# Second feed-forward product by seven block products, with left sums that pass through DRAM

## The chip, the cores and the metric

The kernel runs on one core of a Trainium2 chip. The time is device microseconds for one execution of the whole program. The core's engines are TensorE (PE, with its weight loads PEld), VectorE (DVE), ScalarE (ACT), GpSimd (POOL) and SyncE (SP), whose queue issues nearly all transfers between DRAM and the on-chip memory (SBUF). Matmuls write to eight banks of PSUM.

## What is computed

One encoder block: a mixer (windowed attention and a gated delta rule, side by side), then a feed-forward part with a squared ReLU, then a last RMSNorm. All in float32.

```python
h = h + jnp.concatenate([attn, gdn], axis=-1) @ w_out[l]
hn = _rmsnorm(h, norm_ffn_w[l])
h = h + jnp.square(jax.nn.relu(hn @ w_ffn_in[l])) @ w_ffn_out[l]
return _rmsnorm(h, norm_final_w)
```

There are 1024 tokens, a model width of 1024 and a feed-forward width of 4096. The two feed-forward products take about half of the time; the change lies in the second and in what joins it to the first.

## The kernel before

A float32 product is made of three matmuls. `split` (L111) divides an operand into a high part, a cast by ScalarE (L115), and a low part, the operand less its high part, subtracted by GpSimd (L116). `mm3` (L118) issues high x high, high x low and low x high into one PSUM bank (L120, L121, L122).

The first feed-forward product is already made by seven block products of halves. It runs over 16 groups `g` of 256 feed-forward columns. `columns` makes a group's operands one group ahead (sums S1 to S4 on VectorE, L1016 to L1024, then splits into the tags wh, wl and sc); `pair_products` issues the products P1, P2, P6, P5, P7, P3, P4, each of 12 matmuls of 128x512, so 84 per group. A group's banks are all psA or all psB, by turns. Copies and adds out of PSUM are ScalarE's (L1045) and VectorE's (L1040). Of each group four blocks of 128 feed-forward rows by 512 tokens result; `store_act` (L1048) squares the ReLU of each in one VectorE instruction (L1049) and stores it (L1050) to `ad` in DRAM.

The second product (`ffn2`) runs over 16 groups of 256 feed-forward rows. `load_second` loads a group's two rows of `ad` and two of the weight, 512 KB each (L1093), splits them, and keeps them in tag pg (group 0: in wh, wl and sc, so that it is ready while the first product still runs). For each of eight token tiles and each half of the columns six matmuls follow, and VectorE adds the bank into the residual `h[t]` (L1117). That is 16 x 8 x 2 x 2 x 3 = 1536 matmuls. `h` is loaded from DRAM at the seam (L1235). In the last group `finish` (L1134) normalises and stores each token tile; the last tile has a chain of its own.

Tiles come from pools with a tag and a number of buffers: pg has 28 (of 4 KB a partition), pt 12 (2 KB), wr and sc 4, wh and wl 3, psA and psB 4 banks each. The framework sets each engine's order of instructions at build time, by a timeline that it estimates; on the chip each engine runs its list in order. A transfer on SP waits in that list for the data it stores and for the buffer it fills, and holds those behind it.

Of the kernel before, what the change touches and what calls it, by code (L numbers as in the profile page):

```python
# [30 lines left out]
C_GQ, C_GK, C_GV, C_Z, C_AB = 768, 1280, 1792, 2304, 2816  # L31

# [41 lines left out]
class Block:  # L74
# [987 lines left out]
    def pair_products(self, g, ops):  # L1062
        tag = "psB" if "early" in ops else ("psA", "psB")[g % 2]
# [4 lines left out]
        self.store_act(g, 0, 0, self.add_to(b, p1))  # L1068
# [5 lines left out]
        if "early" in ops:  # L1074
            d, c, x7 = ops["early"]
            self.store_act(g, 1, 1, self.add_to(w, x7))
            self.store_act(g, 0, 1, self.add_to(c, w))
        else:
            d = self.ps(tag)
            self.product(d, ops, "P7")  # L1080
            self.store_act(g, 1, 1, self.add_to(d, w))
# [6 lines left out]
    def load_pair(self, src, mks):  # L1088

        out = []  # L1090
        for i in range(2):
            raw = self.wr((P, D))
            self.nc.sync.dma_start(out=raw, in_=src(i))  # L1093
            h, l = mks[2 * i](dt=F32R), mks[2 * i + 1](dt=F32R)
            for half in range(2):
                sl = slice(half * HALF, (half + 1) * HALF)
                self.split(raw[:, sl], h[:, sl], l[:, sl])
            out.append((h, l))
        return out

    def load_second(self, g):
        m1, m2 = ((self.wh, self.wl, self.sc, self.wh), (self.wl, self.sc, self.wh, self.wl)) if g == 0 else ((self.pg,) * 4,) * 2
        a = self.load_pair(lambda i: self.ad[2 * g + i], m1)
        return a, self.load_pair(lambda i: self.io["w_ffn_out"][0, (2 * g + i) * P:(2 * g + i + 1) * P, :], m2)

    def ffn2(self, a, w2, tiles, last):
        nc = self.nc
        for t in tiles:
            tk = slice(t * P, (t + 1) * P)
            end = last and t == tiles[-1]  # L1110
            ss, rs = self.small((P, 2)), self.small((P, 1))
            halves = [slice(0, HALF), slice(HALF, D)]
            for nh, sl in enumerate(halves):
                ps = self.ps(("psA", "psB")[nh])
                for i in range(2):
                    self.mm3(ps, a[i][0][:, tk], a[i][1][:, tk], w2[i][0][:, sl], w2[i][1][:, sl], i == 0, i == 1)
                nc.vector.tensor_tensor(out=self.h[t][:, sl], in0=self.h[t][:, sl], in1=ps, op=ALU.add)  # L1117
                if end:
                    scr = self.pt((P, HALF), BF16)
                    nc.scalar.activation(out=scr, in_=self.h[t][:, sl], func=AF.Square, accum_out=ss[:, nh:nh + 1])  # L1120
            if end:
                nc.vector.tensor_tensor(out=ss[:, 0:1], in0=ss[:, 0:1], in1=ss[:, 1:2], op=ALU.add)
# [141 lines left out]
```

## Time and profile before

| | us |
|---|---|
| median of three timed runs | 1295.6 (1295.33 to 1300.9) |
| the profiled execution | 1294.7 |
| its span, first to last instruction | 1293.0 |
| TensorE busy | 1244.8 |
| VectorE busy | 820.7 |
| GpSimd busy | 559.7 |
| ScalarE busy | 490.2 |

The first feed-forward product lies at about 630 to 939 us of the span, the second from there to 1285. Busy times are averages over stages of different kinds, so a stage is read by its own window, and a series of matmuls by the distance of their starts: the time of one matmul in the trace overlaps with the next.

### The profile page before, as it was taken

What the parts mean: (1) busy time and instruction counts of PE and PEld (TensorE: products, weight loads), DVE (VectorE), ACT (ScalarE), POOL (GpSimd) and SP (SyncE); (2) the same over time, 40 slices, a digit from 0 to 9 for tenths busy, and PEclk for the clock granted to TensorE, in tenths of its full rate; (3) what the DMA queues carried; (4) which work ended last, traced back from release to release, by engine and by line L of the source; (5) the groups of instructions that cost most, each with busy time, mean ns of one, the idle gap of its engine ahead of it and who ended that gap; (6) DMA issues with size and microseconds to landing.
All of it is one profiled execution on the core that took longest, in us unless ns stands there. A gap on an engine that the chain in (4) does not pass through costs nothing.

```text
span 1293.0 us, 18542 instructions
## 1 busy us (share of the span) xinstructions
PE 1244.8 (96%) x6674; PEld 1005.8 (78%) x6674; DVE 820.7 (63%) x1505; ACT 490.2 (38%) x1119; POOL 559.7 (43%) x490
## 2 busy tenths in 40 slices
PE   6999998999899999999799999999999999999997
PEld 5778776877777778787578888888888888888886
DVE  4667676872489886765886566576355555555556
ACT  6455688145556561215532232232321212121203
POOL 5364222333423242224765554565573636353512
PEclk9999999999899999999899999999999999999999
DMA  6134445424856576132143332332852323232303
GB/s 231 50 120 130 115 155 174 133 77 100 209 162 161 161 277 223 42 106 98 49 139 104 117 111 94 122 107 98 285 195 65 114 82 112 84 103 93 98 1 130
DMA packets 102044, 162.44 MB, mean 126 GB/s; under 512 B 8867, under 2 KB 62240, under 8 KB 101953
## 3 DMA queue, kind: packets, MB, share of 16 engines
q1 hardware_dynamic: 93252, 156.77, 37.5%
q0 software_dynamic: 8448, 4.20, 1.8%
q8 instruction: 52, 0.85, 0.3%
q14 instruction: 39, 0.32, 0.1%
q10 hardware_dynamic: 253, 0.30, 0.1%
HBM read 109.81 MB, written 50.91 MB: 124 GB/s over the span
## 4 chain that ended last, share of the span: by engine, by line
PE 67%; DVE 3%; issue 1%; ACT 1%; DMA 0%; POOL 0%; POOLq 0%; DVEq 0%; ACTq 0%; SPq 0%
PE psA L120 10%; PE psA L122 10%; PE psA L121 10%; PE psB L120 8%; PE psB L122 8%; PE psB L121 8%; PE psB L792 4%; PE psA L580 2%; PE psA L569 2%; PE psA L540 1%; PE psA L541 1%; DVE pt L1040 0%; DMA pg<-in_w_out 0%; DVE pg L211 0%; PE psB L756 0%
## 5 line engine op out<-in xcount | busy, mean ns | idle before, releaser
L116 POOL TENSOR_TENSOR pg<-wr,pg 128x512 fp32r<-128x512 f32 x120 | 151.4, 1299 | 164.5 <-issue 160.4
L120 PE MATMUL psA<-pg,wh 128*128 128x512 f32 x416 | 168.0, 405 | 2.7 <-ACT pt L454 2.1
L122 PE MATMUL psA<-pg,wl 128*128 128x512 f32 x416 | 166.9, 401 | 0.0
L121 PE MATMUL psA<-pg,wh 128*128 128x512 f32 x416 | 166.6, 401 | 0.3 <-POOL pg L945 0.3
L115 ACT CAST pg<-wr 128x512 fp32r<-128x512 f32 x120 | 64.8, 618 | 248.9 <-PE psB L121 234.6
L116 POOL TENSOR_TENSOR wl<-wr,wh 128x512 fp32r<-128x512 f32 x48 | 76.6, 1618 | 160.7 <-ACT wh L115 153.2
L1117 DVE TENSOR_TENSOR pg<-pg,psA 128x512 f32<-128x512 f32 x128 | 87.7, 687 | 82.3 <-PE psA L122 82.3
L1117 DVE TENSOR_TENSOR pg<-pg,psB 128x512 f32<-128x512 f32 x128 | 87.7, 687 | 81.2 <-PE psB L122 81.2
L120 PEld LDWEIGHTS psA<-pg,wh 128*128 128x128 f32 x416 | 79.3, 191 | 22.1 <-ACT pt L454 2.4
L121 PEld LDWEIGHTS psA<-pg,wh 128*128 128x128 f32 x416 | 79.3, 191 | 20.4 <-issue 0.9
L122 PEld LDWEIGHTS psA<-pg,wl 128*128 128x128 f32 x416 | 79.2, 190 | 18.5
L120 PE MATMUL psA<-pg,pg 128*128 128x512 f32 x240 | 93.4, 389 | 0.0
L121 PE MATMUL psA<-pg,pg 128*128 128x512 f32 x240 | 93.4, 389 | 0.0
L120 PE MATMUL psB<-pg,pg 128*128 128x512 f32 x240 | 93.4, 389 | 0.0
L121 PE MATMUL psB<-pg,pg 128*128 128x512 f32 x240 | 93.4, 389 | 0.0
L122 PE MATMUL psA<-pg,pg 128*128 128x512 f32 x240 | 93.4, 389 | 0.0
L122 PE MATMUL psB<-pg,pg 128*128 128x512 f32 x240 | 93.4, 389 | 0.0
L1049 DVE SCALAR_TENSOR_TENSOR pt<-pt 128x512 f32<-128x512 f32 x64 | 90.0, 1407 | 1.1
L115 ACT CAST wh<-wr 128x512 fp32r<-128x512 f32 x80 | 47.0, 623 | 111.7 <-DVE wr L1018 42.7
L116 POOL TENSOR_TENSOR wl<-wr,wl 128x512 fp32r<-128x512 f32 x32 | 53.5, 1673 | 66.3 <-ACT wl L115 66.3
L1040 DVE TENSOR_TENSOR pt<-psA,pt 128x512 f32<-128x512 f32 x39 | 26.7, 686 | 56.1 <-PE psA L122 37.2
L116 POOL TENSOR_TENSOR wh<-wr,wh 128x512 fp32r<-128x512 f32 x32 | 43.1, 1351 | 42.7 <-ACT wh L115 42.7
(374 smaller groups left out, 3024.9 us busy)
## 6 DMA issues: line engine op xcount, KB each, us to landing
wr<-in_w_ffn_in SPq DMA_DIRECT2D x32, 512.0 KB, 3.9
ad<-pt SPq DMA_DIRECT2D x64, 256.0 KB, 2.8
wr<-ad SPq DMA_DIRECT2D x32, 512.0 KB, 3.5
wr<-in_w_ffn_out SPq DMA_DIRECT2D x32, 512.0 KB, 3.6
wr<-in_w_in SPq DMA_DIRECT2D x22, 512.0 KB, 4.8
pg<-in_x SPq DMA_DIRECT2D x16, 512.0 KB, 5.0
sc<-kvd SPq DMA_DIRECT2D x14, 512.0 KB, 4.3
kvd<-pt SPq DMA_DIRECT2D x16, 256.0 KB, 2.7
```

Source lines behind the costliest of these rows:

```text
L115: nc.scalar.copy(out=h, in_=raw)
L116: nc.gpsimd.tensor_tensor(out=l, in0=raw, in1=h.bitcast(F32), op=ALU.subtract)
L120: nc.tensor.matmul(ps, wh, xh, start=first, stop=False, skip_group_check=onto)
L121: nc.tensor.matmul(ps, wh, xl, start=False, stop=False, skip_group_check=onto)
L122: nc.tensor.matmul(ps, wl, xh, start=False, stop=last, skip_group_check=onto)
L540: nc.tensor.matmul(ps[:, :width], q[:, g, :], self.kh[kv][:, keys], start=True, stop=False)
L569: nc.tensor.transpose(ps[:, g, :], tiles[g // 2][:, g % 2, j * P:(j + 1) * P], self.ident)
L580: nc.tensor.matmul(ps[64 * kv:64 * kv + 64, :], self.va[:, kb, 64 * kv:64 * kv + 64], pts[kv][j].rearrange("p g q -> p (g q)"), start=j == ...
L792: nc.tensor.matmul(ps[:, h - g.start, :], left(h), right[:, h, :], start=True, stop=True)
L1040: self.nc.vector.tensor_tensor(out=out, in0=in0, in1=in1, op=ALU.add)
L1049: self.nc.vector.scalar_tensor_tensor(out=c, in0=c, scalar=0.0, in1=c, op0=ALU.max, op1=ALU.mult)
L1117: nc.vector.tensor_tensor(out=self.h[t][:, sl], in0=self.h[t][:, sl], in1=ps, op=ALU.add)
```

## The change

The second product is made by seven block products too. The feed-forward rows are taken in four parts `n` of four groups (k = 0 to 3), the tokens and the output columns in halves. One step is one product of one n: four token tiles x four k x three matmuls, 48. There are 4 x 7 steps, so 1344 matmuls.

The left operands of the seven products are three of the activated blocks (a11, a12, a22) and four sums (s1, s2, s4 and a11 - a21): seven per group. They are made in `pair_products`, where the blocks arise. `act` squares the ReLU by two ScalarE passes in place of the one VectorE instruction, VectorE makes the sums, and `keep` stores the seven blocks to `sd` in DRAM, 256 KB each (four before).

In the second product `second_operands` loads, for each step, four raw left blocks from `sd` into pt, splits them with the subtract on VectorE, and splits the four right ones with the subtract on GpSimd; high and low part now share one pg tile. The right sums T1, T2 (at P6), T3 and N4 (at P5) are made by VectorE, in place over the weights or in pt. The weights come in by eight loads of 512 KB per n, to wr, wh, wl and sc (L1120). `second_products` issues a step's matmuls; P6 goes onto P1's bank, P3 onto P5's and P4 onto P7's. The results are added into `h` by VectorE (L1170); P6 is kept apart in `u2` (copied by ScalarE in n = 0), and in the last n GpSimd adds u2 into three quarters of `h`. `prepare(i + 1)` is written ahead of step i; `prepare(0)` stands behind the last group's `pair_products`. The tile that ends last has its chain in `finish_last`.

```diff
...
-    def store_act(self, g, i, half, c):
-        self.nc.vector.scalar_tensor_tensor(out=c, in0=c, scalar=0.0, in1=c, op0=ALU.max, op1=ALU.mult)
-        self.nc.sync.dma_start(out=self.ad[2 * g + i, :, half * HALF:(half + 1) * HALF], in_=c)
+    def act(self, c):
+
+        self.nc.scalar.activation(out=c, in_=c, func=AF.Relu)
+        self.nc.scalar.activation(out=c, in_=c, func=AF.Square)
+        return c
+
+    def keep(self, g, p, t):
+
+        self.nc.sync.dma_start(out=self.sd[g, SECOND.index(p)], in_=t)
...
-            self.store_act(g, 0, 1, self.add_to(c, u2, self.pt()))
+            a21 = self.act(self.add_to(c, u2, self.pt()))
+        self.keep(g, "P4", a22)
+        s1, s2, s4 = self.pt(), self.pt(), self.pt()
+        v.tensor_tensor(out=s1, in0=a21, in1=a22, op=ALU.add)
+        v.tensor_tensor(out=a21, in0=a11, in1=a21, op=ALU.subtract)
+        v.tensor_tensor(out=s2, in0=s1, in1=a11, op=ALU.subtract)
+        self.keep(g, "P5", s1)
+        self.keep(g, "P7", a21)
+        self.keep(g, "P6", s2)
         self.product(d, ops, "P4", False)
-        self.store_act(g, 1, 0, self.add_to(d, u2))
...
+        a12 = self.act(self.add_to(d, u2))
+        v.tensor_tensor(out=s4, in0=a12, in1=s2, op=ALU.subtract)
+        self.keep(g, "P2", a12)
+        self.keep(g, "P3", s4)
...
+    def second_operands(self, n, w2, p):
...
+        for k in range(4):
+            b = w2[k]
+            raw = self.pt()
+            nc.sync.dma_start(out=raw, in_=self.sd[4 * n + k, SECOND.index(p)])
+            s, t = self.pg((P, 2, HALF), F32R), self.pg((P, 2, HALF), F32R)
+            self.split(raw, s[:, 0], s[:, 1], v)
+            if p == "P6":
+                b["T1"] = b["B11"]
+                v.tensor_tensor(out=b["T1"], in0=b["B12"], in1=b["B11"], op=ALU.subtract)
+                b["T2"] = self.pt()
+                v.tensor_tensor(out=b["T2"], in0=b["B22"], in1=b["T1"], op=ALU.subtract)
+            if p == "P5":
+                b["T3"], b["N4"] = b["B12"], b["B21"]
+                v.tensor_tensor(out=b["T3"], in0=b["B22"], in1=b["B12"], op=ALU.subtract)
+                v.tensor_tensor(out=b["N4"], in0=b["B21"], in1=b["T2"], op=ALU.subtract)
+            self.split(b[SECOND_RIGHT[p]], t[:, 0], t[:, 1])
+            left.append(s)
+            right.append(t)
+        return left, right
+
+    def second_products(self, n, p, left, right, banks, last):
...
+        for i in range(4):
+            ps = banks[bank, i] = self.ps(tag) if tag else banks[bank, i]
+            tk = slice(i * P, (i + 1) * P)
+            for k in range(4):
+                self.mm3(ps, left[k][:, 0, tk], left[k][:, 1, tk], right[k][:, 0], right[k][:, 1],
+                         tag is not None and k == 0, k == 3, tag is None)
+            u2 = self.u2[i // 2][:, i % 2]
+            if p == "P6" and n == 0:
+                nc.scalar.copy(out=u2, in_=ps)
+                continue
...
+            nc.vector.tensor_tensor(out=dst, in0=dst, in1=ps, op=ALU.add)
+            if last and p == "P6":
+                for d in (self.h[i][:, hi], self.h[4 + i][:, hi], self.h[4 + i][:, lo]):
+                    nc.gpsimd.tensor_tensor(out=d, in0=d, in1=u2, op=ALU.add)
+            if last and p in ("P3", "P4"):
+                self.finish(i if p == "P3" else 4 + i)
...
             else:
-                nxt = self.load_second(0)
+                w2 = self.load_second(0)
             self.pair_products(g, cols.pop(g))
...
+        prepare(0)
+        for t in range(NT):
             self.h[t] = self.pg((P, D))
             nc.sync.dma_start(out=self.h[t], in_=self.hd[t])
...
+        self.u2 = [self.pg((P, 2, HALF)) for _ in range(2)]
+        for i, (n, p) in enumerate(steps):
+            if i + 1 < len(steps):
+                prepare(i + 1)
...
+            self.second_products(n, p, *ops.pop(i), banks, last)
```

Three places show how the order moves. Line numbers are those of the file that the rows are from: `split` has its cast in L115 and its subtract in L116 before, in L119 and L120 after. The numbers behind a tag tell its buffers apart.

The first is SP's queue at the seam of the two products. Before, the last three stores of group 15 (L1050) stand among the loads of the second product's groups (L1093):

```order
L1050 DMA ad_68<-pt_1482_8501 128x512
L1093 DMA wr_1537_8742<-ad_68 128x1024
L1050 DMA ad_68<-pt_1484_8531 128x512
L1093 DMA wr_1540_8750<-ad_68 128x1024
L1050 DMA ad_68<-pt_1480_8486 128x512
L1093 DMA wr_1543_8758<-in_w_ffn_out 128x1024
L1093 DMA wr_1546_8766<-in_w_ffn_out 128x1024
L1093 DMA wr_1581_8918<-ad_68 128x1024
```

After, the last seven stores of the first product (L1060) come first, pt_1521 being the last activated block (a12) and pt_1528 the sum s4, and behind them the left loads of P1 and P2 (L1132):

```order
L1060 DMA sd_68<-pt_1526_8731 128x512
L1060 DMA sd_68<-pt_1525_8726 128x512
L1060 DMA sd_68<-pt_1527_8732 128x512
L1060 DMA sd_68<-pt_1521_8681 128x512
L1060 DMA sd_68<-pt_1528_8733 128x512
L1132 DMA pt_1529_8758<-sd_68 128x512
L1132 DMA pt_1532_8766<-sd_68 128x512
L1132 DMA pt_1535_8774<-sd_68 128x512
L1132 DMA pt_1538_8782<-sd_68 128x512
L1132 DMA pt_1551_8808<-sd_68 128x512
L1132 DMA pt_1554_8816<-sd_68 128x512
```

All loads of left operands have moved behind the last store of the first product.

The second is ScalarE at the same place. Before, casts for the second product's groups stand around the last copies out of PSUM (L1045):

```order
L1045 COPY pt_1479_8457<-psB_1477_8443 128x512
L115 CAST sc_1469_8421<-wr_1468_8419 128x512 x2
L115 CAST wl_1472_8429<-wr_1471_8427 128x512 x2
L115 CAST pg_1494_8568<-wr_1493_8566 128x512 x2
L1045 COPY pt_1480_8486<-psB_1477_8443 128x512
L115 CAST wh_1475_8437<-wr_1474_8435 128x512 x2
L115 CAST pg_1497_8576<-wr_1496_8574 128x512 x2
L115 CAST pg_1500_8584<-wr_1499_8582 128x512 x2
L115 CAST pg_1503_8592<-wr_1502_8590 128x512 x2
```

After, the ReLU (L1054) and the square (L1055) of the last blocks come, then the casts of P1, a left and a right one by turns:

```order
L1054 ACTIVATE pt_1523_8696<-pt_1523_8696 128x512
L1055 ACTIVATE pt_1523_8696<-pt_1523_8696 128x512
L1054 ACTIVATE pt_1525_8726<-pt_1525_8726 128x512
L1055 ACTIVATE pt_1525_8726<-pt_1525_8726 128x512
L1054 ACTIVATE pt_1521_8681<-pt_1521_8681 128x512
L1055 ACTIVATE pt_1521_8681<-pt_1521_8681 128x512
L119 CAST pg_1530_8760<-pt_1529_8758 128x512
L119 CAST pg_1531_8761<-wr_1510_8621 128x512
L119 CAST pg_1533_8768<-pt_1532_8766 128x512
L119 CAST pg_1534_8769<-wl_1512_8625 128x512
```

The casts of the first operands, right ones (from the weights in wr and wl) among them, now stand behind the square of the last block.

The third is VectorE there. Before, the last add and relu-square of group 15 are followed by the adds of the second product (L1117):

```order
L1040 TENSOR_TENSOR pt_1484_8531<-psB_1481_8488,pt_1480_8486 128x512
L1049 SCALAR_TENSOR_TENSOR pt_1484_8531<-pt_1484_8531 128x512
L1040 TENSOR_TENSOR pt_1480_8486<-psB_1483_8503,pt_1480_8486 128x512
L1049 SCALAR_TENSOR_TENSOR pt_1480_8486<-pt_1480_8486 128x512
L1117 TENSOR_TENSOR pg_1485_8550<-pg_1485_8550,psA_1507_8600 128x512
L1117 TENSOR_TENSOR pg_1486_8552<-pg_1486_8552,psA_1511_8618 128x512
L1117 TENSOR_TENSOR pg_1487_8554<-pg_1487_8554,psA_1515_8636 128x512
```

After, the last sums of the first product (L1099, L1100, L1106) are followed by low parts of left blocks (L120) and right sums (L1137, L1139, L1142):

```order
L1044 TENSOR_TENSOR pt_1521_8681<-psB_1524_8698,pt_1521_8681 128x512
L1099 TENSOR_TENSOR pt_1525_8726<-pt_1520_8651,pt_1525_8726 128x512
L1100 TENSOR_TENSOR pt_1527_8732<-pt_1526_8731,pt_1520_8651 128x512
L1106 TENSOR_TENSOR pt_1528_8733<-pt_1521_8681,pt_1527_8732 128x512
L120 TENSOR_TENSOR pg_1530_8760<-pt_1529_8758,pg_1530_8760 128x512
L120 TENSOR_TENSOR pg_1533_8768<-pt_1532_8766,pg_1533_8768 128x512
L1137 TENSOR_TENSOR wr_1510_8621<-wr_1510_8621 128x512
L120 TENSOR_TENSOR pg_1536_8776<-pt_1535_8774,pg_1536_8776 128x512
L1139 TENSOR_TENSOR pt_1570_8903<-wh_1511_8623,wr_1510_8621 128x512
L1142 TENSOR_TENSOR wr_1510_8621<-wh_1511_8623,wr_1510_8621 128x512
L1137 TENSOR_TENSOR wl_1512_8625<-wl_1512_8625 128x512
L120 TENSOR_TENSOR pg_1539_8784<-pt_1538_8782,pg_1539_8784 128x512
```

and this goes on up to the low part of P2's last left block (pg_1561) and the first adds out of PSUM (L1170):

```order
L1139 TENSOR_TENSOR pt_1582_8936<-sc_1517_8635,wl_1516_8633 128x512
L1142 TENSOR_TENSOR wl_1516_8633<-sc_1517_8635,wl_1516_8633 128x512
L1143 TENSOR_TENSOR sc_1513_8627<-sc_1513_8627,pt_1574_8914 128x512
L120 TENSOR_TENSOR pg_1561_8834<-pt_1560_8832,pg_1561_8834 128x512
L120 TENSOR_TENSOR pg_1568_8898<-pt_1567_8896,pg_1568_8898 128x512
L1143 TENSOR_TENSOR wh_1515_8631<-wh_1515_8631,pt_1578_8925 128x512
L1170 TENSOR_TENSOR pg_1541_8790<-pg_1541_8790,psA_1563_8840 128x512
L1170 TENSOR_TENSOR pg_1542_8792<-pg_1542_8792,psA_1564_8854 128x512
```

Between s4 and the low part of pg_1561, that included, stand 22 instructions with two inputs in SBUF, where before the adds out of PSUM followed at once.

## Rows read from the trace of the kernel before

**Rows 1.** The page: span, busy time by engine, chain that ended last.
```profile
span 1293.0 us, 18542 instructions
PE 1244.8 (96%) x6674; PEld 1005.8 (78%) x6674; DVE 820.7 (63%) x1505; ACT 490.2 (38%) x1119; POOL 559.7 (43%) x490
...
PE 67%; DVE 3%; issue 1%; ACT 1%; DMA 0%; POOL 0%; POOLq 0%; DVEq 0%; ACTq 0%; SPq 0%
```

**Rows 2.** Windows: us; PE, PEld, DVE, ACT, POOL busy; clock; DMA share; GB/s.
```profile
700.00:800.00 100.00, 100.00 (x432) 80.85 (x431) 63.54 (x65) 26.30 (x45) 52.48 (x35) 1.00 0.33 107
1000.00:1100.00 100.00, 100.00 (x443) 82.81 (x442) 50.28 (x74) 21.35 (x40) 50.27 (x40) 1.00 0.32 100
```

**Rows 3.** Timeline of TensorE, first product: start us, us, instruction.
```profile
758.75 0.39 PE L120 MATMUL psA<-pg,wl 128*128 128x512 f32 x1
...
797.81 0.40 PE L120 MATMUL psA<-pg,wl 128*128 128x512 f32 x1
```

**Rows 4.** Timeline of TensorE, end of the second product.
```profile
1269.87 0.39 PE L120 MATMUL psB<-pg,pg 128*128 128x512 f32 x1
...
1283.47 0.39 PE L120 MATMUL psB<-pg,pg 128*128 128x512 f32 x1
...
1284.61 0.39 PE L122 MATMUL psB<-pg,pg 128*128 128x512 f32 x1
```

**Rows 5.** Groups: busy us, mean ns of one, idle before and releaser.
```profile
L116 POOL TENSOR_TENSOR pg<-wr,pg 128x512 fp32r<-128x512 f32 x120 | 151.4, 1299 | 164.5 <-issue 160.4
...
L115 ACT CAST pg<-wr 128x512 fp32r<-128x512 f32 x120 | 64.8, 618 | 248.9 <-PE psB L121 234.6
...
L1117 DVE TENSOR_TENSOR pg<-pg,psA 128x512 f32<-128x512 f32 x128 | 87.7, 687 | 82.3 <-PE psA L122 82.3
```

**Rows 6.** Groups of VectorE in the first product, 700 to 900 us.
```profile
L1049 DVE SCALAR_TENSOR_TENSOR pt<-pt 128x512 f32<-128x512 f32 x41 | 66.3, 1616 | 0.7
```

**Rows 7.** Timeline of VectorE and GpSimd, where two instructions meet.
```profile
741.52 1.74 POOL L116 TENSOR_TENSOR wl<-wr,wl 128x512 fp32r<-128x512 f32 x1 [4.07 <-ACT wl L115]
...
742.02 1.78 DVE L1049 SCALAR_TENSOR_TENSOR pt<-pt 128x512 f32<-128x512 f32 x1
```

**Rows 8.** Timeline at the seam: TensorE, SP's queue, VectorE.
```profile
938.50 0.39 PE L122 MATMUL psB<-pg,sc 128*128 128x512 f32 x1
938.73 0.39 PE L120 MATMUL psB<-wh,sc 128*128 128x512 f32 x1
...
932.23 0.33 SPq L1050 DMA_DIRECT2D ad<-pt  x1
...
938.93 0.69 DVE L1040 TENSOR_TENSOR pt<-psB,pt 128x512 f32<-128x512 f32 x1 [1.57 <-PE psB L122]
939.65 0.69 DVE L1049 SCALAR_TENSOR_TENSOR pt<-pt 128x512 f32<-128x512 f32 x1
```

**Rows 9.** DMA issues: number, KB of each, median us to landing.
```profile
ad<-pt SPq DMA_DIRECT2D x64, 256.0 KB, 2.8
wr<-ad SPq DMA_DIRECT2D x32, 512.0 KB, 3.5
...
pt<-pd SPq DMA_DIRECT2D x16, 256.0 KB, 5.4
```

**Rows 10.** Windows ahead of the first product: TensorE busy, clock, DMA share, GB/s.
```profile
628.00:630.00 2.00, 0.16 (x2) 0.83 0.00 0
630.00:632.00 2.00, 1.39 (x3) 0.50 0.00 0
632.00:634.00 2.00, 2.00 (x6) 0.50 0.57 165
634.00:636.00 2.00, 2.00 (x5) 0.50 0.28 98
636.00:638.00 2.00, 2.00 (x9) 0.96 0.85 263
```

More of the change, by code (lines that the diff above doesn't have):

```diff
@@ L1062, in pair_products @@
     def pair_products(self, g, ops):
+        v = self.nc.vector
         tag = "psB" if "early" in ops else ("psA", "psB")[g % 2]
@@ L1080, in pair_products @@
             self.product(d, ops, "P7")
[L1081 removed]
+            a22 = self.act(self.add_to(d, w))
             self.product(c, ops, "P3", False)
[L1083 to L1099 removed]
@@ L1101, in load_second @@
[L1101 to L1106, printed above, removed]
-        nc = self.nc
[L1108 to L1122, printed above, removed]
-                self.rstd(ss[:, 0:1], rs)
-                hw, o = self.pt(), [self.pt(), self.pt()]
-                nc.gpsimd.tensor_tensor(out=hw, in0=self.h[t][:, halves[0]], in1=self.w_fin[:, halves[0]], op=ALU.mult)
-                nc.scalar.activation(out=o[0], in_=hw, func=AF.Copy, scale=rs)
-                nc.vector.scalar_tensor_tensor(out=o[1], in0=self.h[t][:, halves[1]], scalar=rs,
-                                               in1=self.w_fin[:, halves[1]], op0=ALU.mult, op1=ALU.mult)
-                for nh, sl in enumerate(halves):
-                    (nc.scalar, nc.sync)[nh].dma_start(out=self.io["out"][0, t * P:(t + 1) * P, sl], in_=o[nh])
-            elif last:
-                self.finish(t)
@@ new lines, in second_operands @@
+    def second_operands(self, n, w2, p):
+        nc, v = self.nc, self.nc.vector
+        left, right = [], []
+        for k in range(4):
[17 more added lines that the diff above has]
+        return left, right
@@ new lines, in finish_last @@
+    def finish_last(self, t, ps):
+        nc = self.nc
+        lo, hi = slice(0, HALF), slice(HALF, D)
+        h = self.h[t]
+        ss, rs = self.small((P, 2)), self.small((P, 1))
+        scr, hw, o = self.pt((P, HALF), BF16), [self.pt(), self.pt()], [self.pt(), self.pt()]
+        nc.scalar.activation(out=scr, in_=h[:, hi], func=AF.Square, accum_out=ss[:, 1:2])
+        nc.gpsimd.tensor_tensor(out=hw[1], in0=h[:, hi], in1=self.w_fin[:, hi], op=ALU.mult)
+        nc.vector.tensor_tensor(out=h[:, lo], in0=h[:, lo], in1=ps, op=ALU.add)
+        nc.scalar.activation(out=scr, in_=h[:, lo], func=AF.Square, accum_out=ss[:, 0:1])
+        nc.vector.tensor_tensor(out=hw[0], in0=h[:, lo], in1=self.w_fin[:, lo], op=ALU.mult)
+        nc.vector.tensor_tensor(out=ss[:, 0:1], in0=ss[:, 0:1], in1=ss[:, 1:2], op=ALU.add)
+        self.rstd(ss[:, 0:1], rs)
+        nc.scalar.activation(out=o[0], in_=hw[0], func=AF.Copy, scale=rs)
+        nc.vector.tensor_scalar(out=o[1], in0=hw[1], scalar1=rs, scalar2=None, op0=ALU.mult)
+        for i, sl in enumerate((lo, hi)):
+            (nc.scalar, nc.sync)[i].dma_start(out=self.io["out"][0, t * P:(t + 1) * P, sl], in_=o[i])
```

52 lines of the change are left out of this document (38 added, 14 removed).

## The prediction

> **What bounds the kernel now.** I read the page first: the span is 1293.0 us, TensorE is busy for 96% of it, and the chain that ended last runs for 67% through its matmuls, with no other engine above 3% [rows 1]. Then the windows: in the first feed-forward product as in the second, TensorE is busy for all 100 us at a granted clock of 1.00, while VectorE has 64 and 50 of 100, ScalarE 26 and 21, GpSimd 52 and 50 [rows 2]. So a matmul taken away there is worth its whole pitch, as long as the other engines and the loads keep up. The busy time of one matmul (0.39) isn't its pitch, since matmuls overlap. The pitch is read from two starts: in the first product the first matmul of a psA tile comes again after two groups, 168 matmuls, 39.06 us later, 0.2325 us each [rows 3]. In the second, two matmuls five token tiles (60 matmuls) apart are 13.60 us apart, 0.2267 us each [rows 4]. What sets the two apart that I can see is the tag of the operands: the faster rows have both in pg.
>
> **Removed: matmuls.** The second product has 16 groups x 8 tiles x 2 halves x 2 x 3 = 1536 matmuls now and 4 x 7 x 4 x 4 x 3 = 1344 after. Of the 1536, group 0's 96 lie in other tags: 96 x 0.2325 + 1440 x 0.2267 = 348.7 us. After, all operands are in pg: 1344 x 0.2267 = 304.6 us. That is **-44.1 us**, and -36.2 if they should go at 0.2325.
>
> **Added beside the first product.** Per group of 19.5 us (84 x 0.2325) the change takes four relu-squares off VectorE, 1.62 us each [rows 6], and puts four sums there; ScalarE gets eight passes, at the 0.62 us of a cast of the same size 5.0 us [rows 5]; three more 256 KB stores go out. By the windows VectorE has 12.4 us per group now, so some 12.4 - 6.5 + 4 x 1.62 = 12.4 at the old price and 8.7 at 0.69; ScalarE 5.1 + 5.0 = 10.1. Both lie under 19.5. The load on the DMA queues goes from 107 GB/s [rows 2] to about 107 + 0.79 MB / 19.5 us = 147. None of it is on the path in steady state: a relu-square isn't a reader of PSUM, so the banks come free as before. VectorE's sums wait for ScalarE's squares, though, and the next group's operand sums (S1) stand behind s4 on VectorE. Where a group's operands are made late, as at the start of the stage, that can show: **+2 us** (0 to 5), an allowance, bounded by four dependent waits of 1.24 us.
>
> **The seam between the products.** Now it costs nothing: the last matmul of the first product starts at 938.50, the next TensorE rows follow at the usual pitch, and VectorE's add and relu-square run beside them [rows 8]. After, the order puts the loads of the first left operands on SP behind the last two stores of group 15, and the casts on ScalarE behind that group's last relu and square, though the blocks loaded are those of groups 0 to 3, long written. From the last matmul of group 15: VectorE's add 0.69 [rows 8], relu and square 2 x 0.62 [rows 5], s4 0.69 [rows 8], the store's issue 0.33 [rows 8], a load's landing 3.5 (2.8 to 5.4, [rows 9]; the 3.5 is a load of the same kind of buffer in this stage): 6.5 us idle. Two casts, left then right: 1.24. Then TensorE doesn't run freely, since the operands come one by one from three engines. VectorE has 22 two-input instructions up to the low part of P2's last left block, 22 x 0.69 = 15.2 us alone. Beside them GpSimd makes eight right low parts of 1.30 [rows 5], and a two-input VectorE instruction that meets one of these waits: the relu-square started at 742.02 took 1.78 and not 0.69 because GpSimd's subtract ran until 743.26 [rows 7]. In the mean over 41 of them it was 1.62, that is 0.93 more [rows 6]. With 8 x 0.93 the queue needs 0.62 + 15.2 + 7.4 = 23.2 us from the landing (15.8 with no meeting, 26.2 with 8 x 1.30). TensorE running freely would want that block at its 57th matmul, 1.24 + 57 x 0.2267 = 14.2. So it waits about 9 us in P1 and P2 (1.6 to 12). Last the clock: after TensorE had been nearly idle from 624 to 630 the granted clock was 0.50 for some 5.5 us of work, that is 1.2 instead of 2.4 GHz [rows 10], which would cost 2.75 us; part of it falls into the waits just named, so 2. Sum: 6.5 + 1.24 + 9 + 2 = **+18.7 us** (9 to 25).
>
> **The second product in steady state.** One n is 336 matmuls, 76.2 us. ScalarE: 56 casts x 0.62 = 34.7. GpSimd: 28 x 1.30 = 36.4. VectorE: 28 adds from PSUM x 0.687 = 19.2, which GpSimd doesn't lengthen (the mean over 128 is 687 ns at a GpSimd busy half of the time, [rows 2, 5]), and 44 two-input instructions, 44 x 0.69 = 30.4, plus 28 x 0.93 = 26.0 for the meetings: 75.6 of 76.2. So TensorE covers it, but only just, and unevenly: the 16 right sums of an n stand in the two steps before its P1 and P2. There VectorE has 27 two-input instructions, eight adds and eight meetings, 18.6 + 5.5 + 7.4 = 31.5 us in two steps of 10.9. What helps is that an add of P4 may be some 8 us late before the next P1 wants its bank (the other three tiles of the step come first), and that the operands have 2.25 steps of pg buffers; I allow 1 us for each of three such places, **+3 us** (0 to 8). Loads are 28 x 0.26 MB + 8 x 0.52 MB = 11.5 MB per n, 151 GB/s, against 100 now [rows 2]; up to 263 GB/s were moved in a window [rows 10]. In the last n GpSimd has 12 adds more, 15.6 us, 52 of 76: covered, and no product but the last ones waits for them.
>
> **The tail.** From the last matmul (1284.61, [rows 4]) to the end are 8.4 us now. finish_last has the same chain behind it, add, square, small sum, rstd, scale, store. I take 0 (-0.5 to +0.5).
>
> **The sum.** On the profiled execution: 1294.7 - 44.1 + 2 + 18.7 + 3 = 1274.3 us. That execution is 0.9 under the median of 1295.6, so **1275 us**. About 0.5% can be told from no change, so faster means under 1289.1 and slower over 1302.1.
>
> **Rivals.**
> *The pitch stays at 0.2325.* The high and low parts will share one pg tile, and if the faster pitch comes from something else than the tag, the second product takes 312.5 us: 1275 + 7.9 = 1283. For it: I have only a correlation. Against it: 1440 matmuls hold the faster pitch.
> *VectorE becomes the bound, and the kernel is slower.* If every one of the 28 right low parts of an n blocks VectorE for its full 1.30 us, an n needs 30.4 + 36.4 + 19.2 = 86.0 us against 76.2, 9.8 x 4 = 39 more, 1275 + 39 - 3 = 1311. It passes the time before from 5 us per n on, a meeting price of 1.11 (75.6 is reached at 0.93). For it: the row at 742.02 lost 1.09. Against it: the waits take turns, GpSimd's subtract is held up too (1.74 instead of 1.30, [rows 5, 7]), so fewer meet, and such a VectorE only meets when both have work. The Trainium skill, page "SBUF — State Buffer", section "Who interferes with whom", has a rule for this: a VectorE instruction with two inputs in SBUF and a GpSimd instruction that reads SBUF take a lock, and the later one blocks in full until the other ends. By that rule the full 1.30 is the most that a meeting costs, and this rival its worst case; the row at 742.02 agrees with the rule, its 1.78 being the rest of GpSimd's 1.74 and 0.6 of its own.
> *The first product slows.* If the chain add, relu, square, sums, S1 of the next group ends last in each of 14 groups by 1 us, 1275 - 2 + 14 = 1287. Against it: operands are made a group ahead, and ScalarE and VectorE have a third of each group free.
> *The seam is cheap.* With no meetings there (wait 1.6, the clock's loss inside it): 1275 - 9.4 = 1266; with a landing in 2.8 us and no other allowance 1260.
>
> **How the numbers follow.** The forecast, seam near 19 us and the rest hidden, 0.54; the slow pitch 0.17; VectorE bound 0.09; the first product 0.08; the cheap seam 0.10; 0.02 for what I haven't thought of. The low end of the range is the cheap seam with its bounds, 1260. The high end takes in the pitch rival and the first product's, and the forecast with seam and allowances at their upper bounds (+6 +3 +5 = 1289): 1289. VectorE bound and half of what lies beyond stay out. Faster: 0.54 + 0.17 + 0.10 + half of 0.08 = 0.85; slower 0.08 of VectorE's 0.09; the rest, 0.07, within 0.5%.
>
> **What would show it.** In the profile after: TensorE idle for 6 to 7 us behind group 15 and then with gaps through P1 and P2, ended by VectorE's low parts, at a granted clock that falls to 0.50; 0.2267 us from matmul to matmul in the second product; VectorE's mean for its left low parts between 0.7 and 1.6 us; gaps of TensorE before P1 and P2 of a new n of a microsecond at most; groups of the first product still 19.5 us apart. The prediction is wrong if TensorE waits for VectorE in every n (then the meetings are dearer), if the first product's groups are longer, or if the seam is hidden.

## The result, and the profile after

The changed kernel takes 1278.05 us in the median (1276.52 to 1282.06), against 1295.8 before: ratio 0.986, 95% interval 0.983 to 0.989. The forecast was 1275 in a range of 1260 to 1289. The profiled execution took 1276.97 us, 17.7 less than that of before.

The page of after, the same parts as [rows 1]: span, busy time, the chain that ended last.

```profile
span 1275.3 us, 18723 instructions
PE 1207.9 (95%) x6482; PEld 972.6 (76%) x6482; DVE 860.6 (67%) x1534; ACT 613.6 (48%) x1347; POOL 580.9 (46%) x486
...
PE 22%; DVE 2%; issue 1%; DMA 0%; ACT 0%; SPq 0%; POOLq 0%; DVEq 0%; POOL 0%
```

192 matmul records have gone. TensorE's busy time fell by 36.9 us and the span by 17.7 only, so idle time has come in somewhere. The waits of TensorE from 620 to 960 us and behind that say where (engine, line, who was waited for, us in total, times, longest):

```profile
PE psA L124 <- ACT pg L119: 9.4, 1, 9.4
PE psB L124 <- ACT pt L1049: 2.6, 1, 2.6
...
PE psB L124 <- DVE pt L1044: 1.4, 1, 1.4
...
PE psA L126 <- DVE pg L120: 4.0, 2, 3.2
PE psB L126 <- DVE pg L120: 3.2, 3, 1.3
```

None of these stood in the trace of before. L1049 and L1044 are the copy and the add out of PSUM in group 15; the others lie at the seam and in the three steps behind it. After 986 us TensorE waits for nothing until its last matmul; this window shows most of that stretch (columns as in [rows 2]):

```profile
1030.00:1240.00 210.00, 210.00 (x928) 173.91 (x927) 175.71 (x199) 82.31 (x154) 136.49 (x85) 1.00 0.39 119
```

The pitches are about those of [rows 3, 4]. In the first product a psA tile's first matmul comes again after two groups, 168 matmuls, 39.13 us later (39.06 before); at the end of the second, 39 matmuls take 8.84 us, 0.2267 each:

```profile
758.39 0.39 PE L124 MATMUL psA<-pg,wh 128*128 128x512 f32 x1
...
797.52 0.39 PE L124 MATMUL psA<-pg,wh 128*128 128x512 f32 x1
...
1257.73 0.39 PE L126 MATMUL psA<-pg,pg 128*128 128x512 f32 x1
...
1266.57 0.39 PE L126 MATMUL psA<-pg,pg 128*128 128x512 f32 x1
```

So the gain is where it was expected, and most of the loss is at the seam. Its timeline, SP's queue, ScalarE, TensorE:

```profile
940.92 3.40 SPq L1060 DMA_DIRECT2D sd<-pt  x5
944.41 4.99 SPq L1132 DMA_DIRECT2D pt<-sd  x9
...
948.63 0.62 ACT L119 CAST pg<-pt 128x512 fp32r<-128x512 f32 x1 [6.12 <-DMA pt<-sd]
...
949.83 2.07 PE L124 MATMUL psA<-pg,pg 128*128 128x512 f32 x4 [9.36 <-ACT pg L119]
...
961.89 0.50 PE L126 MATMUL psA<-pg,pg 128*128 128x512 f32 x1 [3.18 <-DVE pg L120]
```

The last matmul of group 15 started at 940.07; five stores fill SP's queue until 944.32, the first load behind them lands after 4.2 us (to the cast that waits for it), and TensorE starts at 949.83, 9.36 us after it fell idle. Then P1 and P2, 96 matmuls, take until 982.50: 32.7 us for 21.8 us of work. VectorE and GpSimd in that stretch:

```profile
949.28 0.69 DVE L120 TENSOR_TENSOR pg<-pt,pg 128x512 fp32r<-128x512 f32 x1 [6.04 <-ACT pg L119]
...
951.61 1.77 DVE L1137 TENSOR_TENSOR wr<-wr 128x512 f32<-128x512 f32 x1
953.30 1.78 DVE L120 TENSOR_TENSOR pg<-pt,pg 128x512 fp32r<-128x512 f32 x1
955.00 1.78 DVE L1139 TENSOR_TENSOR pt<-wh,wr 128x512 f32<-128x512 f32 x1
...
973.95 3.48 DVE L120 TENSOR_TENSOR pg<-pt,pg 128x512 fp32r<-128x512 f32 x2
...
952.79 1.74 POOL L120 TENSOR_TENSOR pg<-wr,pg 128x512 fp32r<-128x512 f32 x1
954.49 1.75 POOL L120 TENSOR_TENSOR pg<-wl,pg 128x512 fp32r<-128x512 f32 x1
```

From 951 to 963 us each engine starts one instruction every 1.70 us, in turn: a two-input VectorE instruction waits for GpSimd's subtract, and the next subtract for it. VectorE's first line here begins its row of 22 up to P2's last low part; the line of 973.95 holds the 22nd, which ended at 975.73, and one more. The granted clock (windows of TensorE: busy, clock, DMA share, GB/s) falls to 0.50 with the idle time and stays there for some matmuls behind it, as in [rows 10]. It does so behind the wait of 2.6 us in group 15 too (first line). At the seam the DMA engines are full:

```profile
930.00:932.00 2.00, 2.00 (x6) 0.50 1.05 407
...
944.00:946.00 2.00, 0.00 (x0) 0.50 1.05 407
...
950.00:952.00 2.00, 2.00 (x5) 0.50 1.05 402
952.00:954.00 2.00, 2.00 (x7) 0.70 1.07 411
...
964.00:966.00 2.00, 2.00 (x6) 0.50 0.97 361
```

For the experiments I use a second measure beside the median. Ahead of the first product all kernels here run the same instructions in the same order, and yet that part ended between 629.8 and 634.5 us in their profiled executions. So the length from the first matmul of the first product to the last matmul of the second, in the profiled execution, compares better where a few us matter.

| kernel | median us | length us | against the changed kernel |
|---|---|---|---|
| before | 1295.8 | 654.0 | +17.5 |
| changed | 1278.05 | 636.5 | |
| sums_only | 1303.8 | 662.6 | (before + 8.6) |
| loads_ahead | 1277.38 | 636.7 | +0.2 |
| right_dve | 1266.94 | 626.2 | -10.3 |
| act_dve | 1275.98 | 633.6 | -2.9 |
| seam_dve | 1273.24 | 629.5 | -7.0 |
| left_pool | 1306.88 | 656.9 | +20.3 |
| hoist | 1272.54 | 630.7 | -5.8 |
| best | 1263.94 | 623.9 | -12.6 |
| dve_act | 1264.08 | | |
| best_queue | 1260.89 | 617.0 | -19.5 |
| own_queue | 1261.69 | 617.0 | -19.5 |

The profiled execution of dve_act ran at a granted clock of 0.56, so it has no length here.

### The profile page after: what moved, and what is told of

It reads as the page before. It is cut to its first block, busy times and chain, and to the rows that moved or that the text cites. A ratio compares the mean times of both kernels' runs of the same rounds, so it can differ in the third digit from the quotient of the medians.

```text
span 1275.3 us, 18723 instructions
## 1 busy us (share of the span) xinstructions
PE 1207.9 (95%) x6482; PEld 972.6 (76%) x6482; DVE 860.6 (67%) x1534; ACT 613.6 (48%) x1347; POOL 580.9 (46%) x486
## 5 line engine op out<-in xcount | busy, mean ns | idle before, releaser
L119 ACT CAST pg<-pt 128x512 fp32r<-128x512 f32 x128 | 76.4, 617 | 165.9 <-PE psA L126 63.5
L120 DVE TENSOR_TENSOR pg<-pt,pg 128x512 fp32r<-128x512 f32 x112 | 133.9, 1217 | 26.3 <-ACT pg L119 25.6
L120 POOL TENSOR_TENSOR wl<-wr,wh 128x512 fp32r<-128x512 f32 x44 | 70.5, 1625 | 153.6 <-ACT wh L119 153.6
L120 POOL TENSOR_TENSOR wh<-wr,wh 128x512 fp32r<-128x512 f32 x32 | 47.1, 1491 | 141.6 <-ACT wh L119 133.9
L1054 ACT ACTIVATE pt<-pt 128x512 f32<-128x512 f32 x64 | 40.4, 632 | 145.4 <-DVE pt L1044 145.4
L124 PE MATMUL psA<-pg,pg 128*128 128x512 f32 x256 | 100.4, 397 | 9.4 <-ACT pg L119 9.4
L126 PE MATMUL psA<-pg,pg 128*128 128x512 f32 x256 | 100.7, 394 | 4.0 <-DVE pg L120 4.0
L125 PE MATMUL psA<-pg,pg 128*128 128x512 f32 x256 | 100.5, 393 | 0.0
L126 PE MATMUL psB<-pg,pg 128*128 128x512 f32 x192 | 74.9, 391 | 3.2 <-DVE pg L120 3.2
L125 PE MATMUL psB<-pg,pg 128*128 128x512 f32 x192 | 74.7, 389 | 0.0
L124 PE MATMUL psB<-pg,pg 128*128 128x512 f32 x192 | 74.7, 389 | 0.0
L1044 DVE TENSOR_TENSOR pt<-psB,pt 128x512 f32<-128x512 f32 x39 | 26.9, 690 | 63.8 <-PE psB L126 38.2
L1044 DVE TENSOR_TENSOR pt<-psA,pt 128x512 f32<-128x512 f32 x39 | 26.7, 689 | 59.2 <-PE psA L126 42.0
L119 ACT CAST wh<-wr 128x512 fp32r<-128x512 f32 x76 | 43.5, 623 | 45.1 <-PE psA L125 24.5
L124 PEld LDWEIGHTS psA<-pg,pg 128*128 128x128 f32 x256 | 49.0, 192 | 19.9 <-ACT pg L119 9.8
L126 PEld LDWEIGHTS psA<-pg,pg 128*128 128x128 f32 x256 | 48.7, 190 | 15.5 <-DVE pg L120 5.3
```

What stands on the lines that cost most here:

```text
L120: (eng or nc.gpsimd).tensor_tensor(out=l, in0=raw, in1=h.bitcast(F32), op=ALU.subtract)
L124: nc.tensor.matmul(ps, wh, xh, start=first, stop=False, skip_group_check=onto)
L125: nc.tensor.matmul(ps, wh, xl, start=False, stop=False, skip_group_check=onto)
L126: nc.tensor.matmul(ps, wl, xh, start=False, stop=last, skip_group_check=onto)
L1044: self.nc.vector.tensor_tensor(out=out, in0=in0, in1=in1, op=ALU.add)
L1054: self.nc.scalar.activation(out=c, in_=c, func=AF.Relu)
```

## The experiments

My theory after the comparison: the seam costs by three things, the queue ahead of the first loads (9.4 us idle), the turns that VectorE and GpSimd take in P1 and P2 (10.9 us), and a last group in which ScalarE's copy stands behind its squares (2.6 us). The rival on the second point: VectorE simply has too many instructions there.

### The first product's part alone: sums_only

To the kernel before, `act`, the four sums and their stores are added; the second product stays.

```diff
-        self.store_act(g, 0, 0, self.add_to(b, p1))
+        a11 = self.act(self.add_to(b, p1))
+        self.half(g, 0, 0, a11)
...
+        v.tensor_tensor(out=s1, in0=a21, in1=a22, op=ALU.add)
+        a31 = self.pt()
+        v.tensor_tensor(out=a31, in0=a11, in1=a21, op=ALU.subtract)
+        v.tensor_tensor(out=s2, in0=s1, in1=a11, op=ALU.subtract)
...
+        v.tensor_tensor(out=s4, in0=a12, in1=s2, op=ALU.subtract)
```

> The kernel before with the changed first product alone: relu and square on ScalarE, four sums a group on VectorE, four more stores a group (eight in all, where the change has seven); the second product as before, from its own buffer, and the sums are read by nobody. My theory: the first product hides this work except at its last group, where in the changed kernel TensorE waited 2.6 us for ScalarE's copy and 1.4 us for an add behind it, so 1297 to 1300 us, 1 to 4 over the kernel before. Rival: the sums and the longer chain cost in every group (1 us each), then 1309 or more.

Measured: 1303.8 us, ratio to before 1.0075 (1.0049 to 1.010), more than expected. TensorE's waits from 900 to 960 us:

```profile
PE psB L120 <- ACT pt L1045: 2.0, 1, 2.0
PE psA L120 <- DVE pg L1143: 1.8, 1, 1.8
PE psA L121 <- POOL wl L116: 1.8, 1, 1.8
PE psB L120 <- ACT sc L115: 0.9, 1, 0.9
```

6.6 of the 8.6 us are waits at the seam, and the groups ahead of it are 0.1 us longer each (19.6 for 19.5). So the rival falls: the sums cost 0.1 us a group and not 1. But the longer chain isn't free at the end of the stage, even where the second product waits for no sum.

### The first loads ahead of the last stores: loads_ahead

```diff
+        if g == DFF // 256 - 1:
+            self.raws = [self.raw_left(0, j, "P1") for j in range(4)]
         self.product(d, ops, "P4", False)
...
-            raw = self.pt()
-            nc.sync.dma_start(out=raw, in_=self.sd[4 * n + k, SECOND.index(p)])
+            raw = self.raws[k] if (n, p) == (0, "P1") else self.raw_left(n, k, p)
```

> The changed kernel, with the four left loads of the first step issued ahead of the last two stores of group 15; nothing else moves. My theory: 6 of the 9.4 us in which TensorE stands idle at the seam are the SP queue (stores waiting for their data, their issues, then the landing); with the blocks there, ScalarE's casts follow its last square at once, so the idle time falls to about 3.5 us and the total to about 1272. Rival: what paces the seam is VectorE's row of instructions behind it, and P1 and P2 end when that ends; it starts earlier too, so this rival only says that part is lost again: 1274 to 1276. Second rival: the loads only find buffers late, and nothing changes, 1278.

Measured: 1277.4 us. SP's queue, ScalarE and TensorE's waits:

```profile
942.80 0.96 SPq L1129 DMA_DIRECT2D pt<-sd  x2
...
947.56 0.62 ACT L119 CAST pg<-pt 128x512 fp32r<-128x512 f32 x1 [3.60 <-DMA pt<-sd]
...
PE psA L124 <- ACT pg L119: 6.8, 1, 6.8
PE psB L126 <- DVE pg L120: 5.2, 3, 1.9
```

The idle time fell by 2.5 us only, not by 6: the loads still stood behind a sum's store, and ScalarE's cast of the first came 4.8 us after its issue, in a stretch in which the DMA engines are full. And what was won was lost: P1 and P2 take 36.7 us and not 32.7. TensorE's waits for VectorE's low parts there are 6.9 us for 6.4, but 34 matmuls for 17 start at the lower clock, 0.43 us apart, and lose 6.6 us for 3.3. The time is the same; length +0.2. That is the first rival's mechanism: VectorE's row sets when P2 ends. Its last low part for P2 ended 35.3 us behind the start of group 15's last matmul here, and 35.7 in the changed kernel.

### No GpSimd in the second product: right_dve, seam_dve

right_dve gives the right low parts to VectorE in all steps; seam_dve in P1 and P2 of the first n alone.

```diff
-            self.split(b[SECOND_RIGHT[p]], t[:, 0], t[:, 1])
+            self.split(b[SECOND_RIGHT[p]], t[:, 0], t[:, 1], v)
```

```diff
-            self.split(b[SECOND_RIGHT[p]], t[:, 0], t[:, 1])
+            self.split(b[SECOND_RIGHT[p]], t[:, 0], t[:, 1], v if n == 0 and p in ("P1", "P2") else None)
```

> The changed kernel with the right low parts too subtracted on VectorE, in all steps, so that GpSimd does none in the second product. My theory: at the seam VectorE and GpSimd hold each other up (1.7 us for an instruction of either by turns), so that without GpSimd VectorE's row, though it has eight instructions more up to P2's last block (30 x 0.6 to 0.69 = 18 to 21 us), ends earlier than now (about 23 us from its start to P2's last low part); P1 and P2 take 26 to 29 us in place of 32.7, total 1271 to 1275. In steady state VectorE has 72 x 0.65 + 19 = 66 of 76 us and TensorE has no gaps. Rival, VectorE's count of instructions decides: eight more make the seam longer by 5 us and each n's VectorE the bound at its first steps: 1283 or more.

Measured: 1266.9 us, ratio to before 0.978 (0.976 to 0.980), better than expected. VectorE's row at the seam of right_dve, and TensorE's waits there:

```profile
951.09 0.68 DVE L120 TENSOR_TENSOR pg<-wr,pg 128x512 fp32r<-128x512 f32 x1
951.69 0.69 DVE L120 TENSOR_TENSOR pg<-pt,pg 128x512 fp32r<-128x512 f32 x1
952.29 0.68 DVE L1137 TENSOR_TENSOR wr<-wr 128x512 f32<-128x512 f32 x1
...
PE psA L124 <- ACT pg L119: 9.8, 1, 9.8
PE psB L124 <- ACT pt L1049: 2.6, 1, 2.6
```

Eight instructions more, one every 0.60 us and not every 1.70, and no wait for a low part is left. From TensorE's start at 951.02 to its last matmul at 1256.96 are 305.9 us; 1344 matmuls at 0.2267 are 304.7. So the theory of the turns holds, and the rival, that the count decides, falls.

> The changed kernel with the right low parts subtracted on VectorE in the first two steps alone (eight instructions); in the 26 later steps GpSimd has them as before. My theory after right_dve: all of its 11 us lie in P1 and P2 of the first n, where VectorE and GpSimd alternate at 1.7 us for each of their instructions, and nothing in the later steps: 1266 to 1269, as right_dve. Rival: meetings cost in every n too, hidden in TensorE's pitch or in short gaps; then this one gives back a part, 1270 to 1275.

Measured: 1273.2 us. It gives back 7.0 us of length and not 10.3: P1 and P2 run without a wait for a low part, and the turns come a step later, in P6, where TensorE waits 3.1 us for low parts (three times). This is the rival's side of the expectation as to the number, though not as to the place: in the later n no wait appears. GpSimd's first subtract in seam_dve shows something else:

```profile
959.30 9.65 POOL L120 TENSOR_TENSOR pg<-pt,pg 128x512 fp32r<-128x512 f32 x1 [40.09 <-ACT pg L119]
...
967.10 0.68 DVE L1143 TENSOR_TENSOR sc<-sc,pt 128x512 f32<-128x512 f32 x1
967.71 0.68 DVE L1170 TENSOR_TENSOR pg<-pg,psA 128x512 f32<-128x512 f32 x1
968.30 1.19 DVE L1139 TENSOR_TENSOR pt<-sc,wl 128x512 f32<-128x512 f32 x1
```

It started into a run of two-input VectorE instructions, each 0.60 us after the last, and took 9.65 us; it ended 1.24 us after VectorE began to read from PSUM (L1170), about its time alone. So engines that meet don't always take turns: here an unbroken run of the one kept the other out. Every trace read here has another such case near 244 us, in the mixer: there a subtract that starts into a run of smaller two-input VectorE instructions takes 6.7 to 7.8 us (6.90 in the changed kernel, in which 17 instructions of VectorE that started later ran ahead of it), and ends 1.2 us behind the run's last.

### All of it on GpSimd: left_pool

```diff
-            self.split(raw, s[:, 0], s[:, 1], v)
+            self.split(raw, s[:, 0], s[:, 1])
```

> The changed kernel with the left low parts subtracted on GpSimd too, 56 an n, so that VectorE has 16 two-input instructions and 28 adds from PSUM. Theory of meetings (a two-input VectorE instruction and a GpSimd subtract don't run at once): an n needs 56 x 1.28 + 16 x 0.6 = 81 us of the two engines by turns against TensorE's 76, 5 x 4 = 20 more, and the seam is longer, 16 low parts of 1.28 ahead of P2's end and not 8: 1295 to 1310. Rival, the engines only share or the counts alone decide: GpSimd needs 71.7 of 76.2 us and VectorE 30: 1275 to 1285.

Measured: 1306.9 us, slower than before, ratio 1.0088 (1.0068 to 1.011).

```profile
PE psA L124 <- DVE pg L1170: 21.1, 4, 10.4
PE psA L124 <- ACT pg L119: 9.5, 1, 9.5
...
DVE wr L1137 <- POOL pg L120: 9.2, 2, 8.8
```

The number is as the theory of meetings gave it, by a somewhat other way. GpSimd is full in the later windows (68.8 of 70 us from 1140 to 1210), its subtract takes 1.39 us and not 1.30, so an n takes 56 x 1.39 = 78 us and not 81; of the 21.1 us, 17 fall in the first two n (6.6 and 10.4), where VectorE's sums wait for GpSimd and the adds out of PSUM stand behind them. That the number came out is partly luck. P1 and P2 take only 2.0 us more than in the changed kernel (34.7 for 32.7), so nearly all of the loss lies behind the seam. Another 7.6 us are lost behind the last matmul (16.3 for 8.7), which the theory didn't have.

### Relu and square back on VectorE: act_dve

```diff
-        self.nc.scalar.activation(out=c, in_=c, func=AF.Relu)
-        self.nc.scalar.activation(out=c, in_=c, func=AF.Square)
+        self.nc.vector.scalar_tensor_tensor(out=c, in0=c, scalar=0.0, in1=c, op0=ALU.max, op1=ALU.mult)
```

> The changed kernel with relu and square again in one VectorE instruction in the place of two ScalarE passes. My theory: the wait of 2.6 us of TensorE in group 15 came from ScalarE's copy standing behind the squares of group 14, and goes, and the seam's chain is shorter by 0.6 us (one instruction of 0.69 for two of 0.63): 1274 to 1276. Rival: VectorE, which meets GpSimd in the first product (1.6 us a relu-square) and has the sums now too, becomes late in every group: 1285 or more.

Measured: 1276.0 us, as expected, though against the changed kernel that is within what runs differ by. In the trace the wait for L1049 is gone and nothing takes its place; the first product is 305.6 us long and not 310.0, so VectorE isn't late there. 2.6 of these 4.4 us are the wait, and 1.6 the matmuls at the lower clock behind it (up to 932.81). At the seam 1.5 of the 4.4 us are lost again.

### The operands of the first step made beside the first product: hoist, best

Group 15 makes P7 and P3 first, so that operand buffers come free, and `prepare(0)` moves ahead of its `pair_products`. best has right_dve and act_dve too.

```diff
                 w2 = self.load_second(0)
+                for _ in self.early(cols[g]):
+                    pass
+                prepare(0)
             self.pair_products(g, cols.pop(g))
...
-        prepare(0)
```

> The changed kernel, but group 15 makes P7 and P3 first, as groups 0 and 1 do, so that eight operand buffers come free early, and the first step's operands are loaded and split while group 15 runs; meetings stay. My theory: the idle time of 9.4 us at the seam goes nearly all, and the low parts of P1 are made beside the first product; P2's row of VectorE and GpSimd is still paced by meetings, so 3 to 6 of the 11 us in P1 and P2 stay: 1263 to 1269. Rival: as with loads_ahead, what is won at the seam is lost in P1 and P2 behind the same row of VectorE: 1274 or more.

> Three edits together: group 15 makes P7 and P3 first and the first step's operands are made beside it (hoist), all low parts of the second product are VectorE's (right_dve), relu and square are one VectorE instruction (act_dve). My theory: the gains add, since they lie in three places, 9 at the seam's idle time, 11 in P1 and P2, 4 in the first product (its length was 310.0 us in the changed kernel and 305.6 in act_dve): 1278 - 24 = 1254, between 1251 and 1259. Rival: VectorE, which then has most of the work beside TensorE, is late in P2 of the first n and takes back a part: 1260 to 1266.

Measured: 1272.5 us in hoist, between its two ranges and nearer the rival's, and 1263.9 in best, in its rival's. The seam itself lost its gap, 2.1 us idle in hoist and none in best, but a wait of 7.5 and 9.6 us stands ahead of P2. In best, SP's queue, ScalarE and TensorE:

```profile
948.46 8.13 SPq L1059 DMA_DIRECT2D sd<-pt  x5
956.64 0.44 SPq L1131 DMA_DIRECT2D pt<-sd  x1
...
960.64 0.62 ACT L119 CAST pg<-pt 128x512 fp32r<-128x512 f32 x1 [17.87 <-DMA pt<-sd]
...
961.83 2.08 PE L124 MATMUL psB<-pg,pg 128*128 128x512 f32 x4 [9.55 <-ACT pg L119]
```

The rival of best named VectorE, and it is SP: P2's left loads stand behind five stores of group 15, and these wait for VectorE's last sums, which the order puts behind adds of P1. The wait had only moved from the first step to the second.

### The loads on a queue of their own: dve_act, best_queue, own_queue

dve_act is right_dve with act_dve. best_queue is best, own_queue is dve_act, and in both the left loads of P1 and P2 of the first n go out on GpSimd's queue, and P2's operands are written ahead of the loads of `h`.

```diff
-            nc.sync.dma_start(out=raw, in_=self.sd[4 * n + k, SECOND.index(p)])
+            (nc.gpsimd if n == 0 and p in ("P1", "P2") else nc.sync).dma_start(out=raw, in_=self.sd[4 * n + k, SECOND.index(p)])
...
+        prepare(1)
         for t in range(NT):
             self.h[t] = self.pg((P, D))
```

> right_dve and act_dve together: in the second product all low parts on VectorE, in the first relu and square in one VectorE instruction; the loads stay where they are. My theory: two places, two gains, 11 from P1 and P2 and 4 from the first product (310.0 to 305.6 us), so 1262 to 1264, and TensorE idle for 9 us at the seam as before. Rival, VectorE is late where it has both: 1267 or more.

> The kernel best, in which TensorE went through the seam without a gap but then stood idle for 9.6 us ahead of P2 of the first n, since P2's left loads stood in SP's queue behind group 15's last stores (948.5 to 956.6) and those behind VectorE; here the eight left loads of P1 and P2 go out on GpSimd's queue, which has nothing else there, and the 4 MB of the residual are issued after them. My theory: the 9.6 us go but for 1 to 3, 1254 to 1258. Rival, the DMA engines are the limit there (share 1.0, 400 GB/s, from 935 to 955 in best) and the loads land as late whatever queue they stand in: 1262 or more.

> dve_act with the eight left loads of P1 and P2 of the first n on GpSimd's queue, and P2's operands written ahead of the loads of the residual; group 15 keeps its order. The loads are free of SP's stores, so the blocks lie there when group 15 ends, and the casts wait only for operand buffers, which P3 of group 15 gives back 2.8 us before its end. My theory: TensorE's idle time falls from 9 to 2 to 4 us and nothing is lost behind it, since VectorE is quick enough there: 1255 to 1259. Rival, DMA engines at the limit: 1261 or more.

Measured: 1264.1, 1260.9 and 1261.7 us. The first is as expected. The other two lie some 3 us above the expected ranges, own_queue in that of its rival, the DMA engines at their limit; part of that is the stretch ahead of the first product, 2.5 and 3.8 us longer in their profiled executions than in that of the changed kernel. Their lengths are both 617.0, 6.9 under best and 9.2 under right_dve. In the medians the queue is worth less, 3.1 us from best and 2.4 from dve_act, and the runs of own_queue and dve_act overlap (1259.9 to 1262.9 and 1260.2 to 1265.1). So its gain rests on the traces. TensorE's waits in own_queue, and the landing of the eight loads on GpSimd's queue (median, us):

```profile
PE psA L125 <- DVE pg L120: 4.6, 2, 2.5
...
PE psB L124 <- DVE pt L1044: 1.4, 1, 1.4
PE psA L124 <- ACT pg L119: 0.4, 1, 0.4
...
pt<-sd POOLq DMA_DIRECT2D x8, 256.0 KB, 6.4
```

The idle time at the seam is 0.4 us. So SP's queue was what held the first loads. Behind that, 4.6 us wait for low parts, which my theory had at nothing, and matmuls at the lower clock lose another 1.2. There the full DMA engines may well have a part: the eight loads took 6.4 us to land, against 3.0 in the median of the changed kernel's 112 left loads, and VectorE stood 3.1 us until a sum's store had landed. What lighter traffic would give isn't shown. In best_queue the edit also moves P2's loads ahead of the residual's, and the two aren't told apart; in the changed kernel they were ahead already. Both are the fastest here by their medians: ratio to before 0.974 (0.972 to 0.976), where dve_act has 0.975 (0.973 to 0.977).

## Why the prediction was right

**The matmuls, -44.1: right.** 1344 at 0.2267; the rival of the slow pitch fell, with high and low part in one pg tile. From the first matmul of P6 (982.50) to the last are 284.1 us for 1248, of which 1.4 over the pitch are P6's (12.3 us for 10.9).

**The first product, +2: inside its bounds (0 to 5), the place wrong.** I put it at the start, in groups whose operands are made late. The groups keep 19.5 us up to the last ones. What came is in group 15. Counted by the starts of the matmuls it is 6.0 us: waits of 2.6 and 1.4 us idle, 1.6 for matmuls at the lower clock behind the first, and 0.4 around the waits. The copy of P1 out of PSUM stands on ScalarE behind group 14's squares, which wait for VectorE's add, and P6 goes onto the bank that the copy reads; the 1.4 is an add behind a copy that waited for a pt buffer, until a sum's store had landed. act_dve took the 2.6 away, and the 1.6 with it. I had counted ScalarE's time and not what its order makes a copy wait for. On the other side a wait that cost before 1.4 us near 669 is gone. That leaves 4.6 us.

**The seam, +18.7: the path right, the sum 3.1 short, and some of its terms right only together.** Idle time: 6.5 + 1.24 = 7.7 forecast, 9.36 measured (9.5 by the starts). The chain of add, relu, square and s4 ran as worked out (940.50 to 943.24); the rest is SP, 1.2 us from s4's end to the first load's issue where I had 0.33 for one store (five stood there), and 4.2 us from there to the first cast where I had a landing of 3.5, inside the bounds given.

P1 and P2: 9 for the row of VectorE and 2 for the clock, 11 together, 10.9 measured. But the parts are others: 7.5 us go in the waits for low parts (6.4 of them idle), and 3.3 in matmuls at the lower clock. VectorE's row of 22 took 26.4 us (949.28 to 975.73), where I had 15.2 + 7.4 = 22.6. Alone it would be quicker than I had it, 22 x 0.60 = 13.2 us. But twelve subtracts of GpSimd fall into it and not eight, since four of P6's right low parts come before P2's last left one; the other 13.2 us are 1.1 for each of the twelve, where I had 0.93 from [rows 6]. Against that, TensorE first wants P2's last low part at its 68th matmul and not at the 57th, as I had counted. That these errors cancel is luck. That the turns of VectorE with GpSimd are the cause, right_dve shows: without them P1 and P2 take 23.3 us. The 1.4 us in P6 the forecast left out. Together 9.5 + 10.9 + 1.4 = 21.8.

**The later steps, +3: too much.** No gap stands there. VectorE was forecast at 75.6 of 76.2 us an n and measured at 175.7 of 210, that is 63.8. Two terms were mis-sized. VectorE starts a two-input instruction every 0.60 us when nothing holds it, not every 0.69. And with 28 adds of 0.68 there remain 44.7 us for the 44 two-input instructions; less 44 x 0.60 that is 18.3 us for 28 meetings, some 0.65 each by this estimate and not 0.93. Why a meeting costs less here than the 1.1 at the seam isn't shown. Hence the rival "VectorE becomes the bound" was far off with this division of work; left_pool shows that GpSimd becomes it with the other, by some 2 us an n.

**The tail, 0:** 8.7 us from the last matmul's start for 8.4.

Together: -44.1 + 4.6 + 21.8 = -17.7, against -17.5 in the length; 0.2 us stay unexplained. With the tail's +0.3 and a first product that began 0.55 us earlier the length gives the spans' -17.7. The forecast's 1275 is 3 us low. It was 2.6 us short in the first product and 3.1 at the seam, and the 3 us allowed for the later steps, where nothing came, made up for more than half of that. So the number is closer than its terms, and that is luck too.

## What to carry to other kernels

Where one product follows another, look up what stands ahead of the first loads in the queue's order, not only whether their data are ready: here blocks written more than 200 us before waited for the last sum of the last group. Where two engines can't read at once, count the row of the one that the matmuls wait for, one by one, at its start; a mean over a stage tells nothing there, and moving all low parts to one engine won 11 us here though that engine's count of instructions rose. And when a gap goes, ask what the next step's loads stand behind: the gap of the first step came back in the second until those loads had a queue of their own.

## What the runs showed of the hardware

- Matmuls with both operands in tag pg have a pitch of 0.2267 us and those of the first product, with operands in pg and another tag, one of 0.2325 to 0.2329, before and after the change alike. Why isn't shown.
- A GpSimd subtract that started into an unbroken run of two-input VectorE instructions took 9.65 us in seam_dve, and another near 244 us took 6.7 to 7.8 us in each of the traces read (1.30 alone). The Trainium skill, page "SBUF — State Buffer", section "Who interferes with whom", says that whoever issues first holds the shared pair of ports for the whole instruction and the other blocks in full. The turns at the seam agree (1.70 us from one instruction of an engine to its next, with one of the other's between); in seam_dve the pair wasn't given up between instructions either: by the trace thirteen two-input VectorE instructions that started after the subtract ran ahead of it, until VectorE read PSUM, which the order of issue alone doesn't give.
- At the seam of the changed kernel the DMA engines moved 400 GB/s at a share of about 1.0 for nearly 20 us. The nine left loads of 256 KB issued there from 944.4 to 949.4 took 5.7 us to land in the median, against 3.0 over all 112 of the kernel.
- TensorE's granted clock fell to 0.50, the lower of its two levels (1.2 GHz), with the idle time of 9.4 us at the seam, and behind single waits of 2.6 us in group 15 and 3.2 us in P1. Behind each of the three, matmuls started 0.43 us apart for a while.
